# A gated linear unit on one core: the first input tile loaded in one transfer instead of two

## The chip, the cores and the metric

The kernel runs on one core of one Trainium2 chip. The metric is the device time of one execution in microseconds (us). A core has a ScalarE (ACT), a VectorE (DVE), a GpSimd (POOL), a SyncE (SP) and 16 DMA engines that carry data between the chip's memory and the core's on-chip memory. TensorE has no work here.

## The reference

```python
# x: 8192 x 8192, float32
a, b = np.split(x, 2, axis=-1)
return a * (1 / (1 + np.exp(-b)))        # 8192 x 4096, float32
```

So 268.44 MB are read, 134.22 MB are written, and each output element costs one sigmoid and one multiplication.

## The kernel before, in words

The 8192 rows are cut into 32 tiles of 256 rows. In a tile each of the 128 partitions holds two neighbouring rows, so that one partition's share is 64 KB in a row in memory: a tile is 8.39 MB of input and 4.19 MB of output. There are two input buffers (`x_sb0`, `x_sb1`) and two output buffers (`o_sb0`, `o_sb1`); tile i uses buffer i modulo 2 (`SLOTS = 2`).

Three queues set the order of the work, and each is followed strictly in program order, since the helper `place` drops the framework's own dependencies, keeps only the named ones and pins the order:

- **Loads** are issued by SP (`load`, L63). A load of tile i+2 waits for the multiplications of tile i, which had the same input buffer.
- **Sigmoids** run on ACT (L82), in place on the b half of the input buffer.
- **Stores** are issued by ACT too (`store`, L68), in the same queue as the sigmoids. A store waits for the multiplications of its part.

The multiplications (L84) run on VectorE, and for a small share of each tile from tile 2 on, on GpSimd.

`loads`, `works` and `stores` say, tile by tile, into which pieces each step is cut, in eighths of a tile's two rows: (0, 4) is the first row of every partition, (4, 8) the second. A usual tile is loaded and stored whole, and worked in two pieces: 3/16 of the columns of both rows, then the other 13/16. Tile 0 is different: it is loaded in two transfers, one for each row of the pair, worked in four pieces of half a row, and stored in two transfers, one for each row. The last tile is worked in four pieces and stored in three.

`behind[i]` holds stores back in ACT's queue: with 0, the store of the first part stands right behind the sigmoid whose piece completes it; with 1, one further sigmoid is put ahead of that store. Before the change only the last tile has 1.

After the pieces of tile i the load of tile i+2 is issued, then whatever store of tile i is left. For tiles 1 to 31 the first sigmoid also waits until the store of tile i-2 has landed, since it frees the output buffer; the last tile's multiplications wait for that instead, and tile 0 has nothing to wait for but its load.

`_launch_early` moves the first load instruction ahead of the core's opening barrier, so that it is the first thing that SP does; the later loads follow behind the barrier. `_close_on_sync` shortens the closing barrier.

Of the kernel before, what the change touches and what calls it, by code (L numbers as in the profile page):

```python
# [8 lines left out]
def _tiles(ctx, tc, x, out):  # L9
    nc = tc.nc  # L10
    P = nc.NUM_PARTITIONS
    DEP = mybir.DependencyInfo(mybir.DependencyClass.Sync, mybir.DependencyReason.DATA)
    fp32 = mybir.dt.float32
    SIG = mybir.ActivationFunctionType.Sigmoid

    n_rows, n_cols = x.shape
    half = n_cols // 2
    R = 2
    SLOTS = 2
    n_tiles = n_rows // (P * R)  # L20
    x_g = x.rearrange("(g p h r) m -> g h p (r m)", p=P, h=2, r=R)
    out_g = out.rearrange("(g p h r) m -> g h p (r m)", p=P, h=2, r=R)

    pool = ctx.enter_context(tc.tile_pool(name="io", bufs=1))
    xs = [pool.tile([P, R * n_cols], fp32, name=f"x_sb{k}") for k in range(SLOTS)]
    os = [pool.tile([P, R * half], fp32, name=f"o_sb{k}") for k in range(SLOTS)]

    whole = [(0, 8)]
    rows = [(0, 4), (4, 8)]
    cut = half // 16 * 3  # L30
    few_and_most = [(0, 8, 0, cut), (0, 8, cut, half)]
    fourths = [(k, k + 2, k % 4 * half // 4, (k % 4 + 2) * half // 4) for k in range(0, 8, 2)]
    loads = [whole] * n_tiles
    works = [few_and_most] * n_tiles
    stores = [whole] * n_tiles
    behind = [0] * n_tiles
    loads[0] = stores[0] = rows
    works[0] = works[-1] = fourths
    stores[-1] = [(0, 4), (4, 6), (6, 8)]
    behind[-1] = 1  # L40

    def meet(a, b):
        return a[0] < b[1] and b[0] < a[1]

    traced = [[] for _ in range(SLOTS)]
    load_of, mul_of, store_of = {}, {}, {}

    def place(i, ins, *needs):


        kept = {n.ins.name for n in needs}
        for e in traced[i % SLOTS]:
            if e.ins.name not in kept:
                tc.declare_no_dep(ins.ins, e.ins, reason="follows from the waits that are kept")
        traced[i % SLOTS].append(ins)
        tc.keep_in_program_order(ins)
        return ins

    def load(i):
        for lo, hi in loads[i]:  # L60
            c = slice(lo * n_cols // 4, hi * n_cols // 4)
            free = [m for w, m in mul_of.get(i - SLOTS, []) if meet(w, (lo, hi))]
            ins = nc.sync.dma_start(out=xs[i % SLOTS][:, c], in_=x_g[i // 2, i % 2, :, c])  # L63
            load_of.setdefault(i, []).append(((lo, hi), place(i, ins, *free)))

    def store(i, lo, hi):
        c = slice(lo * half // 4, hi * half // 4)
        ins = nc.scalar.dma_start(out=out_g[i // 2, i % 2, :, c], in_=os[i % SLOTS][:, c])  # L68
        done = [m for w, m in mul_of[i] if meet(w, (lo, hi))]
        store_of.setdefault(i, []).append(((lo, hi), place(i, ins, *done)))  # L70

    def work(i, lo, hi, near, far):

        rows = xs[i % SLOTS].rearrange("p (r h m) -> p r h m", r=R, h=2)
        packed = os[i % SLOTS].rearrange("p (r m) -> p r m", r=R)
        r, c = slice(lo // 4, (hi + 3) // 4), slice(near, far)
        b = rows[:, r, 1, c]
        landed = [s for w, s in load_of[i] if meet(w, (lo, hi))]
        gone = [s for w, s in store_of.get(i - SLOTS, []) if meet(w, (lo, hi))]
        by_sigmoid = 0 < i < n_tiles - 1  # L80
        needs = [*landed, *(gone if by_sigmoid else ())]
        sig = place(i, nc.scalar.activation(out=b, in_=b, func=SIG), *needs)  # L82
        engine = nc.gpsimd if far == cut and i > 1 else nc.vector
        mul = engine.tensor_mul(out=packed[:, r, c], in0=rows[:, r, 0, c], in1=b)  # L84
        if by_sigmoid:
            for s in gone:
                tc.add_manual_dep(sig.ins, s.ins.name, DEP, reason="frees the output slot")
        place(i, mul, sig, *(() if by_sigmoid else gone))
        mul_of.setdefault(i, []).append(((lo, hi), mul))

    for i in range(SLOTS):
        load(i)
    for i in range(n_tiles):
        due = list(stores[i])
        for k, piece in enumerate(works[i]):
            work(i, *piece)
            ready = works[i][k - behind[i]][1] if k >= behind[i] else 0
            while len(stores[i]) > 1 and k < len(works[i]) - 1 and due[0][1] <= ready:
                store(i, *due.pop(0))
        if i + SLOTS < n_tiles:  # L100
            load(i + SLOTS)
        for lo, hi in due:
            store(i, lo, hi)
# [71 lines left out]
@with_exitstack  # L175
def kernel(
    ctx: ExitStack,
    tc: tile.TileContext,
    x: bass.AP,
    out: bass.AP,  # L180
):
    nc = tc.nc
    with ExitStack() as pools:
        _tiles(pools, tc, x, out)
    tc.close()
    tc.compile()
    _launch_early(nc)
    _close_on_sync(nc)
# [30 lines left out]
```

## Time and profile before

| | |
|---|---|
| time, median of 3 runs | 932.53 us (932.44 to 932.56) |
| the profiled execution, its own time | 932.5 us |
| its span in the profile | 931.1 us |
| instructions in the span | 325 |
| busy: VectorE, ACT, GpSimd | 25%, 25%, 11% of the span |
| read, written | 268.44 MB, 134.22 MB |
| mean DMA rate over the span | 432 GB/s |

Times in the profile count from the start of the span; the 1.4 us between the span and the execution's time lie outside of what is recorded. A queue is named by its issuer: q1 carries the loads that SP issues, q10 the stores that ACT issues. A DMA's "landing" is the moment at which its completion is seen by whoever waits for it. The profile's packets are the pieces into which a transfer is split for the DMA engines.

### The profile page before, as it was taken

The numbers are of one execution on the slowest core, as the hardware profiler recorded it, in microseconds if no ns is written. First come the engines' busy times: TensorE is split into PE (matmuls) and PEld (weight loads), VectorE is DVE, ScalarE is ACT, GpSimd is POOL, SyncE is SP. The second block draws the span as 40 slices with busy tenths as digits, with TensorE's granted clock in tenths as the row PEclk, the third lists the DMA queues.
The fourth block names the chain that finished last, engine by engine and source line by source line (L and its number), as shares of the span: only waits on it lengthen the run. The fifth ranks groups of instructions, "written<-read, shape, count | busy, mean of one in ns | idle before, by whom it ended". The sixth has DMA issues, their size and how long they took to land.

```text
span 931.1 us, 325 instructions
## 1 busy us (share of the span) xinstructions
DVE 232.5 (25%) x39; ACT 229.8 (25%) x69; POOL 99.9 (11%) x33
## 2 busy tenths in 40 slices
DVE  1133311333113331133320333203332033320233
ACT  2123332033320333203332023320233302333023
POOL 0001111011110111101111011110111101111010
DMA  9999999999999999999999999999999999999998
GB/s 405 450 439 417 428 450 424 455 405 428 450 428 450 407 469 409 428 450 427 452 405 450 428 428 450 424 452 408 428 450 428 450 408 465 411 428 450 427 452 383
DMA packets 9793, 402.67 MB, mean 432 GB/s; under 512 B 1088, under 2 KB 1088, under 8 KB 1088
## 3 DMA queue, kind: packets, MB, share of 16 engines
q1 hardware_dynamic: 4752, 268.44, 66.6%
q10 hardware_dynamic: 5040, 134.22, 33.4%
q14 instruction: 1, 0.01, 0.0%
HBM read 268.44 MB, written 134.22 MB: 432 GB/s over the span
## 4 chain that ended last, share of the span: by engine, by line
DMA 75%; DVE 12%; ACT 12%; issue 0%; ACTq 0%; SPq 0%
DMA out_dram<-o_sb 65%; DVE o_sb L84 12%; ACT x_sb L82 12%; DMA x_sb<-in_x_dram 10%; ACTq L68 0%; SPq L63 0%
## 5 line engine op out<-in xcount | busy, mean ns | idle before, releaser
L84 DVE TENSOR_TENSOR o_sb<-x_sb 128x6656 f32<-128x6656 f32 (+2 forms) x39 | 232.5, 5970 | 690.2 <-ACT x_sb L82 690.2
L82 ACT ACTIVATE x_sb<-x_sb 128x1536 f32<-128x1536 f32 (+1 forms) x68 | 228.5, 3407 | 689.9 <-DMA out_dram<-o_sb 630.0
L84 POOL TENSOR_TENSOR o_sb<-x_sb 128x1536 f32<-128x1536 f32 x29 | 99.7, 3437 | 787.7 <-ACT x_sb L82 787.7
L82 ACT ACT_TABLE_LOAD x1 | 1.3, 1283 | 0.8 <-PEq L203 0.8
L203 POOL MEMSET const-float32-0.0<- 128x1 f32 x1 | 0.1, 98 | 0.2 <-issue 0.2
L203 POOL MEMSET const-bfloat16-1.0<- 128x1 bf16 x1 | 0.1, 101 | 0.0
L203 POOL MEMSET const-uint8-127<- 128x1 uint8 x1 | 0.1, 101 | 0.0
L203 POOL MEMSET const-float32-1.0<- 128x1 f32 x1 | 0.1, 98 | 0.0
## 6 DMA issues: line engine op xcount, KB each, us to landing
out_dram<-o_sb ACTq DMA_DIRECT2D x30, 4096.0 KB, 43.6
x_sb<-in_x_dram SPq DMA_DIRECT2D x2, 4096.0 KB, 16.4
out_dram<-o_sb ACTq DMA_DIRECT2D x3, 2048.0 KB, 28.0
out_dram<-o_sb ACTq DMA_DIRECT2D x2, 1024.0 KB, 8.3
x_sb<-in_x_dram SPq DMA_DIRECT2D x31, 43.5
```

Source lines behind the costliest of these rows:

```text
L82: sig = place(i, nc.scalar.activation(out=b, in_=b, func=SIG), *needs)
L84: mul = engine.tensor_mul(out=packed[:, r, c], in0=rows[:, r, 0, c], in1=b)
L203: nc = _bacc.Bacc("TRN2", target_bir_lowering=False, num_devices=1)
```

## The change

```diff
     stores = [whole] * n_tiles
     behind = [0] * n_tiles
-    loads[0] = stores[0] = rows
+    stores[0] = rows
+    behind[0] = 1
     works[0] = works[-1] = fourths
```

Tile 0 is now loaded whole, in one transfer of 8.39 MB in place of two of 4.19 MB. Its four pieces of work and its two stores stay. With `behind[0] = 1`, the store of its first row stands behind the third sigmoid of tile 0 in ACT's queue, where it stood behind the second. `_launch_early` takes the first load that it finds, which is now the whole tile. Nothing else in the program's order is different: SP has one instruction less, and on ACT the third sigmoid and the first store change places.

## The prediction

> **What bounds the kernel now.** I read the page's DMA rows first, then the timeline of the first 75 us, then the DMA issues one by one with their time to landing, and the end of the trace last.
>
> ```profile
> DMA  9999999999999999999999999999999999999998
> DMA packets 9793, 402.67 MB, mean 432 GB/s; under 512 B 1088, under 2 KB 1088, under 8 KB 1088
> q1 hardware_dynamic: 4752, 268.44, 66.6%
> q10 hardware_dynamic: 5040, 134.22, 33.4%
> ```
>
> The two queues fill 66.6% + 33.4% = 100% of the 16 DMA engines' span. No slice is empty, not even the first or the last. So the bound is the number of bytes, and an edit that keeps the bytes can cost time only if it lets the DMA engines run dry, or changes how long they take for a piece.
>
> The piece: 33 loads made 4752 packets, 144 each. All 68 transfers made 1088 tiny ones, 16 each (completions). So a transfer is 128 data pieces, eight for each DMA engine, one for each partition.
>
> ```profile
> 11.98 3.71 ACT L82 ACTIVATE x_sb<-x_sb 128x2048 f32<-128x2048 f32 x2 [9.91 <-DMA x_sb<-in_x_dram]
> 18.45 0.37 ACTq L68 DMA_DIRECT2D out_dram<-o_sb  x1
> 21.68 3.71 ACT L82 ACTIVATE x_sb<-x_sb 128x2048 f32<-128x2048 f32 x2 [5.99 <-DMA x_sb<-in_x_dram]
> 23.62 4.49 DVE L84 TENSOR_TENSOR o_sb<-x_sb 128x2048 f32<-128x2048 f32 x2 [5.21 <-ACT x_sb L82]
> 28.15 0.36 ACTq L68 DMA_DIRECT2D out_dram<-o_sb  x1
> 46.29 7.12 ACT L82 ACTIVATE x_sb<-x_sb 128x1536 f32<-128x1536 f32 x2 [20.90 <-DMA x_sb<-in_x_dram]
> 60.57 0.36 ACTq L68 DMA_DIRECT2D out_dram<-o_sb  x1
> 70.71 7.12 ACT L82 ACTIVATE x_sb<-x_sb 128x1536 f32<-128x1536 f32 x2 [17.30 <-DMA out_dram<-o_sb]
> ```
>
> Rows 0 and 1 of tile 0 land at 11.98 and 21.68, tile 1 at 46.29; tile 2 starts at 70.71, and what it waits for is a store. The DMA issues at 18.45, 28.15 and 28.15:
>
> ```profile
> out_dram<-o_sb ACTq DMA_DIRECT2D x1, 2048.0 KB, 28.0
> ...
> out_dram<-o_sb ACTq DMA_DIRECT2D x1, 2048.0 KB, 42.5
> x_sb<-in_x_dram SPq DMA_DIRECT2D x1, 42.3
> ```
>
> Store 0a (first row of tile 0) lands at 18.45 + 28.0 = 46.4, just as load 1 does. Store 0b and load 2 land at 28.15 + 42.5 = 70.7 and 70.5. Load and store land in pairs although one is 8.39 MB and the other 2.10: an engine takes one piece from each queue in turn. A pair of these takes 70.5 - 46.3 = 24.2 us (10.49 MB, 433 GB/s), a pair of load and whole store 99.66 - 70.71 = 28.95 us (12.58 MB, 435 GB/s). Hence, over eight pieces, 0.6 us for a 16 KB store piece, 1.2 for 32 KB, 2.42 for a 64 KB load piece. The trace's packet records have 0.611, 1.213 and 2.418. These three durations carry the rest.
>
> In the steady state a tile's sigmoids and products (99.66 to 113.99) take 14.33 us of each 28.95 us, and the DMA has the other buffer's 28.95 us queued meanwhile. That is 14.6 us of cover.
>
> **The change part by part.**
>
> *One load for two.* Per DMA engine, sixteen 32 KB pieces of 1.213 us (19.41) become eight of 64 KB at 2.418 (19.34), with one completion less (0.01): **-0.07 us** of DMA time. The first pieces are slow (1.67 to 2.02 us in the packet records, some 0.6 us of warm-up); the new first piece should pay the same, and I bound the difference by 0.3 us either way, half of it.
>
> *The wait that is added.* No part of tile 0 can start before 21.68 - 0.07 = 21.61. The first sigmoid, first product and store 0a, which had 11.98, 13.92 and 18.45, now queue behind a wait of 9.6 us more. On ACT: sigmoids at 21.61, 23.4 and 25.2, the third done at 27.1. Store 0a waits for product 2, which ended at 23.62 + 4.49 = 28.11 where it followed the same landing: issue at 28.15 - 0.07 = 28.08, **9.6 us later**. Behind it on ACT stands sigmoid 4: 28.08 + 0.37 of issue + 0.04 = 28.5, done 30.4. Product 4 takes 30.4 to 32.7, and load 2 on SP and store 0b on ACT leave at 32.75, **4.6 us later** than 28.15. What hides both delays is load 1, which runs from about 21.2 to beyond 40.
>
> *What is late next.* The question is whether the DMA engines have work at every moment. The ledger, in work per engine: loads 0 and 1 last until 1.0 (first piece) + 0.6 + 2 x 19.34 = 40.3. Load 2 and store 0 (29.0 us) are in the queue by 32.75 and carry it to 69.3. Load 3 and store 1 are issued when tile 1 is done: load 1 lands earlier than 46.29, near 42.8, because it shares with fewer store pieces, and 42.8 + 14.3 = 57.1. They carry it to **98.6**. Then load 4 and store 2 must be there, issued when tile 2 is done, and tile 2 waits for all of store 0. This is the one tight place.
>
> *When store 0 lands.* The load queue is never empty meanwhile, so its 16 pieces alternate with 64 KB ones. Before, its first piece started at 23.6 and tile 2's sigmoid at 70.71, 47.1 us later; that distance stays. So I need only when the first piece of store 0a gets in. It can only do so between load 1's pieces, which begin at about 21.1, 23.5, 25.9, 28.4, 30.8, **33.2, 35.6, 38.0**. Before, it got in 5.1 us after issue, with three load pieces started in between (18.7, 19.9, 21.1 in the packet records). If the delay is a time, or so many bytes already taken in hand, 28.08 + 5.1 gives 33.2. If it is three pieces whatever their size, 35.6. One more piece would be 38.0. I take 33.2, the answer of two of the readings, and keep the others.
>
> From 33.2: tile 2's sigmoid at 80.3 (before: 70.71), load 4 and store 2 issued 14.33 later at 94.65. The first load's piece started 1.0 us after its issue, so they are at the engines by 95.7, 2.9 us before these run dry. **Cost 0.** From 35.6: 82.7, 97.05, 98.05, and with 0.6 us of warm-up 98.65 against 98.6: cost 0 to 0.1, up to 1.3 if a start takes 2.2 us instead of 1.0.
>
> *After that.* Load 3 and store 1 have landed by 98.6, or some pieces later where load 4 mixes in, at worst about 104; 14.3 us on, load 5 and store 3 are issued by 118, and the queue holds until 127.6. From there the old rhythm with its cover. At the end, the last load lands at 911.66 and the first store of tile 31 goes out at 918.13, 6.5 us later; store 30's 9.7 us cover that with 3.2 us to spare. Loads that run a little ahead of stores leave more stores for the end, so this cover grows.
>
> **Sum:** span 931.1 - 0.07 = 931.0; with the 1.4 us outside it, 932.4 against this execution's 932.5. Against the median 932.53: **932.46 us**.
>
> [...]
>
> **The rivals.**
>
> *Slower: the DMA engines run dry at 98.6.* Price: the first piece of store 0a at 38.0 puts tile 2 at 85.1, load 4 and store 2 at 99.45, their first pieces at 100.45; 1.85 us dry and 0.6 of warm-up, 2.5 us: **934.9**. It decides from a first piece later than about 36. For it: the delay was 5.1 us where a bare start took 1.0, so pieces are taken in hand ahead of time, and these are now twice as long. Against: it needs 9.9 us of delay.
>
> *Faster: a transfer has a fixed cost in DMA time.* Row 0 landed at 11.98, row 1 only 9.70 later; if the 2.28 us difference were paid by every transfer in line, one less gives **930.2**. Against: 4.19 MB in 9.70 us are 432 GB/s, the mean of the span, so nothing was paid between the two.
>
> *Slower by the whole delay.* The chain of waits starts with compute on tile 0, and 9.6 us of later start would be **942.1**. It needs DMA engines that idle; the ledger leaves no such place beyond 98.6.
>
> *The change does nothing to the order.* SP's list in the new build has one load of 128x16384 for two of 128x8192, and ACT's three sigmoids ahead of the first store. So it does what it says.
>
> **How the numbers follow.** First piece at 33.2: 0.55, 932.46. At 35.6: 0.29, 932.5 to 933.8. At 38.0: 0.12, 934.9. Whole delay: 0.01. Fixed cost saved: 0.03. Taking 0.2% (1.9 us) as what a measurement of this kernel can tell from no change, the first two are the same: same 0.84, slower 0.13, faster 0.03. The range takes in these two with the warm-up's bound: 932.1 to 934.0; what it leaves out is 0.16.
>
> **What would show it.** Right: one load issue less and 144 packets less on q1 (4608); tile 0's first sigmoid at 21.6, tile 1's near 42.8 (before 46.29), tile 2's near 80.3 or 82.7 (before 70.71), still waiting for a store; no empty DMA slice around 98. Wrong: tile 2 at 85 or later and a gap in DMA there; or a last load that lands with less than 6.5 us of stores behind it, which would open a gap at the end.

## The result, and the profile after

The changed kernel takes **951.73 us** (median of six executions, 950.62 to 960.37), the kernel before 932.58 on the same chip: 19 us slower where no change was forecast, a ratio of 1.0218 over all executions (95% interval 1.0203 to 1.0233; the two medians alone give 1.0205). The profiled execution is the longest of the six (960.37, span 959.0; the other five lie between 950.6 and 952.3), so its profile shows the loss some 9 us larger than usual.

From the page of the changed kernel, the lines that answer to those shown of before:

```profile
DMA  9999999999999999999999999999999999999996
GB/s 435 415 437 408 425 429 424 428 425 422 413 436 428 424 414 427 420 429 415 428 428 416 432 425 406 421 418 435 420 422 428 418 425 426 413 420 426 418 424 294
DMA packets 9649, 402.67 MB, mean 420 GB/s; under 512 B 1072, under 2 KB 1072, under 8 KB 1072
q1 hardware_dynamic: 4608, 268.44, 66.9%
q10 hardware_dynamic: 5040, 134.22, 32.5%
```

The page of before has this for the rate:

```profile
GB/s 405 450 439 417 428 450 424 455 405 428 450 428 450 407 469 409 428 450 427 452 405 450 428 428 450 424 452 408 428 450 428 450 408 465 411 428 450 427 452 383
```

The same bytes, 144 packets less on q1, and DMA engines as busy as before, but at 420 GB/s in place of 432. The loss is spread over the whole span; only the last slice (294) stands out. Two equal stretches from the middle of the kernels, in the table by windows (DVE, ACT and POOL busy, clock, share of the DMA engines, GB/s); first before, then after:

```profile
320.00:900.00 580.00, 141.85 (x20) 142.44 (x40) 68.72 (x20) 1.00 1.00 434
```

```profile
320.00:900.00 580.00, 140.22 (x20) 135.32 (x38) 65.33 (x19) 1.00 1.00 422
```

The share is 1.00 in both: the engines never ran out of work there, so pieces took longer. In the view of the waits this shows as one line that grew by 28.8 us, 1 us for each tile; first before, then after:

```profile
ACT x_sb L82 <- DMA out_dram<-o_sb: 630.0, 29, 22.1
ACT x_sb L83 <- DMA out_dram<-o_sb: 658.8, 29, 29.2
```

The timeline of the start, against the lines that the prediction shows:

```profile
21.98 5.51 ACT L83 ACTIVATE x_sb<-x_sb 128x2048 f32<-128x2048 f32 x3 [19.92 <-DMA x_sb<-in_x_dram]
...
28.45 0.38 ACTq L69 DMA_DIRECT2D out_dram<-o_sb  x1
...
33.13 0.36 ACTq L69 DMA_DIRECT2D out_dram<-o_sb  x1
45.39 7.12 ACT L83 ACTIVATE x_sb<-x_sb 128x1536 f32<-128x1536 f32 x2 [14.61 <-DMA x_sb<-in_x_dram]
...
81.72 7.12 ACT L83 ACTIVATE x_sb<-x_sb 128x1536 f32<-128x1536 f32 x2 [29.21 <-DMA out_dram<-o_sb]
...
96.05 0.36 ACTq L69 DMA_DIRECT2D out_dram<-o_sb  x1
```

Each of these steps came within 2.6 us of the forecast, and nothing ran dry at 98.

**Which pieces took longer.** The trace's packet records give each piece's duration. A load piece that takes longer than 2.418 us is called stretched here. Summed and divided by 16 engines, pieces took 931.4 us before and 953.0 after. 22.0 us of the latter are load pieces beyond their 2.418 us (1.0 before); store pieces are 0.6 us beyond theirs. The stretch begins with load 4 or 5 and is 0.5 to 1.0 us for each tile, mostly in the second and third of a load's eight pieces. The records are followed from the end of one piece to the start of the next, which tells the 16 engines apart. The starts of one load on the engines, 0.3 to 0.6 us apart through all of before, drift from 1.3 us apart (load 4) to 11.6 (load 31). So at the end engines that are ahead have nothing to do while the landing waits for the last one: in the windows table of after,

```profile
925.00:938.00 13.00, 0.00 (x0) 0.00 (x0) 0.00 (x0) 1.00 0.99 429
938.00:946.00 8.00, 4.52 (x3) 5.51 (x3) 0.00 (x0) 1.00 0.41 176
```

Up to 9 us of an engine's time are lost in that gap, 4.9 us in the mean. 21.5 us of longer pieces and 4.9 of gaps make 26.4 of the 27.9 by which the span grew.

**What differs in the queues.** The records of one engine at the border of two tiles (start in us; L and S are load and store pieces, Lm and Sm the 9 ns completion markers, a dash the next tile's):

```
before  240.17 L   242.58 S   243.79 Lm  243.80 Sm  243.80 L'  246.22 S'  247.43 L'
after   126.12 S   127.33 Lm  127.34 S   128.55 L'  130.96 Sm  130.97 L'  133.40 S'  134.60 L' (3.32 us)
```

In these records an engine goes to the other queue after each piece, where that queue has work; what it takes from one queue before it does so is called a turn here. A marker uses up a turn like a piece: at 127.33 the load's marker, at 127.34 the store's next piece. Before, both transfers end in the same pair and the next two begin together. After, the load's marker has used up a turn, the next load is already at its first piece when the store's last has gone, and from there on **loads stand one turn ahead of stores**, on 11 of the 16 engines at load 5. As a number: the last piece of the store ends 1.2 us behind that of the load in before, and 2.4 us behind it in after (median of the engines, each tile from 4 to 30). The other five engines keep the order of before (1.2 us) up to the last tiles, and they are not spared: from load 9 on their load pieces lose 19 to 23 us, those of the eleven 14 to 17. So what slows a piece is not decided by the order of its own engine's two queues alone; the loss is on all 16 engines. The five are also the late ones of the 11.6 us. In the runs rows_behind1 and whole_behind0 below, where all 16 engines stand one turn ahead, load pieces lose 16.8 and 17.3 us and the gap at the end is 1.2 and 0.8.

### The profile page after: what moved, and what is told of

It is laid out like the page before. It is cut to its first block, busy times and chain, and to the rows that moved or that the text cites. A ratio compares the mean times of both kernels' runs of the same rounds, so it can differ in the third digit from the quotient of the medians.

```text
span 959.0 us, 324 instructions
## 1 busy us (share of the span) xinstructions
DVE 232.5 (24%) x39; ACT 229.8 (24%) x69; POOL 99.9 (10%) x33
## 2 busy tenths in 40 slices
DMA packets 9649, 402.67 MB, mean 420 GB/s; under 512 B 1072, under 2 KB 1072, under 8 KB 1072
## 4 chain that ended last, share of the span: by engine, by line
DMA 75%; DVE 12%; ACT 12%; issue 0%; ACTq 0%; SPq 0%
DMA out_dram<-o_sb 66%; DVE o_sb L85 12%; ACT x_sb L83 12%; DMA x_sb<-in_x_dram 9%; ACTq L69 0%; SPq L64 0%
```

## The experiments

Theory at first: load 4 reached the engines just as store 1 ended (99.4 us), and this meeting set the engines on two different orders. Rivals: the large first transfer sets them apart; or loads ahead of stores are enough. In the diffs `...` leaves out what is unchanged.

**Half of the change, and three ways around the meeting.** rows_behind1 has only the second half:

```diff
     loads[0] = stores[0] = rows
+    behind[0] = 1
```

> The kernel before with only the second half of the change: tile 0 is still loaded in two rows, and its first store stands behind the third sigmoid. Store 0a leaves some 5 us later than before (near 23.6), so stores run about three pieces behind loads, alike on all engines; load 4 leaves near 90 and the load queue is never empty. Theory (after the change the load queue ran empty while store 1 still ran, load 4 reached the engines just as store 1 ended at 99.4, and the engines went on in two different orders): no such meeting here, 932.5 us, pieces not stretched. Rival 'the large first transfer sets the engines apart from the start': also 932.5. Rival 'loads that run ahead of stores by a fixed number of pieces are enough': stretched pieces, 945 to 955.

951.64 us (ratio 1.0205, 1.019 to 1.022). The first store left at 21.82 and got in at 26.2 instead of 23.6: one load piece later. Loads stand one turn ahead (2.4 us) from tile 3 on; 16.8 us of stretched pieces. In load 4, whose first pieces still start within 0.3 us of each other, the stretch has begun (0.4 us), so the drift of the engines follows it and doesn't cause it. No large first load, no meeting, the same loss: the theory of the meeting and the rival of the first load fall.

whole_whole stores tile 0 whole too:

```diff
-    stores[0] = rows
-    behind[0] = 1
```

> The changed kernel, but tile 0 is also stored whole (and behind[0] is 0 again): store 0 leaves near 33 in pieces of 32 KB, gets in with about one piece of load 1 to go, and lands near 66. Tile 2 then waits for its load, not for store 0, near 71, load 4 leaves near 86 and the load queue is never empty. Theory (the meeting of load 4 with the end of store 1 divides the engines): no meeting, 932.5. Rival 'the large first transfer sets the engines apart': as the changed kernel, 950 to 952. Rival 'a fixed lead of loads over stores is enough': here stores lead by about a piece, so it expects 932.5 unless a lead of either kind counts.

934.62 us (1.002, 1.0011 to 1.0029). Loads come out three turns behind stores (store's end 8.5 us before the load's), and the waits say the same: all 32 are for loads.

```profile
ACT x_sb L81 <- DMA x_sb<-in_x_dram: 692.8, 32, 22.1
```

1.8 us of stretched pieces, nearly all at the start. The 2 us that it is slower are a gap of its own: the last load lands late (its sigmoid starts at 915.81, before at 911.66), store 30 is gone at 921 on most engines, and the first store of tile 31 leaves at 922.28.

tile2_short works tile 2 in fourths (`works[2] = fourths`), tile2_long puts one more instruction on ACT in tile 2:

```diff
+        extra = []
+        if i == 2 and far == half:
+            a = rows[:, r, 0, c]
+            extra = [place(i, nc.scalar.activation(out=a, in_=a, func=mybir.ActivationFunctionType.Copy), *needs)]
         sig = place(i, nc.scalar.activation(out=b, in_=b, func=SIG), *needs)
...
-        place(i, mul, sig, *(() if by_sigmoid else gone))
+        place(i, mul, sig, *extra, *(() if by_sigmoid else gone))
```

> The changed kernel with tile 2 worked in fourths on VectorE alone, as tile 0 is: load 4 and store 2 leave some 3 us earlier after tile 2's first sigmoid (near 92.7 instead of 96.05) and reach the engines near 96, while store 1 still has some three pieces to go. Theory (it is the coincidence of load 4's arrival with store 1's end that divides the engines): all engines take the same order, 932.5 to 933.5. Rival 'the large first transfer': 950 to 952. Rival 'a fixed lead of loads is enough': loads still lead by a piece, 945 to 955.

> The changed kernel with one more ACT instruction in tile 2, a copy in place of the a half (5.73 us, as the sigmoid of that shape): load 4 and store 2 leave near 101.8 and reach the engines near 105, when they have been dry since 99.5, so all restart together. Theory: 5.5 us dry and 0.6 of warm-up, no stretched pieces afterwards, 938 to 939, so more work makes the kernel faster than the changed one. Rival 'the large first transfer': the loss stays and the delay comes on top, 951 to 957. Rival 'a fixed lead of loads is enough': the restart takes the lead away, 938 to 939 too.

tile2_short: 951.73 us, loads one turn ahead, 16.1 us stretched: a second miss for the meeting. tile2_long: 937.04 us (1.0048). The engines ran dry at 99.2 for 2 to 3 us (5.5 were expected), restarted together with load and store in the same pair (1.2 us), and no later tile is stretched. **More work on ACT made the changed kernel 15 us faster.** What is left of the three is the order of the two queues.

whole_behind0 has the other half of the change alone (tile 0 loaded whole, `behind[0]` stays 0).

> The first half of the change alone: tile 0 is loaded whole and behind[0] stays 0. Store 0a still waits for product 2 and leaves near 28.3, load 2 and store 0b near 35. Theory (it is the late first store, by whatever edit, that puts loads a turn ahead of stores): loads end one turn ahead, as with both halves, 948 to 955. Rival 'the third sigmoid ahead of the first store is what does it': 932.5 to 934.

952.63 us, one turn ahead, 17.3 us stretched. Either half alone costs what both cost.

**Shifting the queues by one marker.** In the middle of a kernel one transfer is split in two across the partitions, which keeps bytes and pieces and adds a marker to its queue. Of before_cut_store8 (before_cut_load10, after_cut_load6 and after_cut_store6 differ in the tile and in which of the two queues):

```diff
+    load_cut, store_cut = None, 8
+    def cuts_of(i, tile):
+        return [slice(0, 112), slice(112, P)] if i == tile else [slice(0, P)]
...
-        ins = nc.scalar.dma_start(out=out_g[i // 2, i % 2, :, c], in_=os[i % SLOTS][:, c])
+        for p in cuts_of(i, store_cut):
+            ins = nc.scalar.dma_start(out=out_g[i // 2, i % 2, p, c], in_=os[i % SLOTS][p, c])
```

> The kernel before, with one edit in its middle: the store of tile 8 goes out as two transfers, of partitions 0 to 111 and 112 to 127, the same bytes and still eight data pieces for each engine, but one more completion marker (9 ns) in the store queue. If markers take turns as pieces do, stores fall one turn behind loads from there on, as after the change. Theory 'loads one turn ahead of stores': from about tile 10 on load pieces are stretched by 0.5 to 0.8 us a tile and the engines drift apart, 943 to 951. Rival 'the way in which tile 0 starts': no effect, 932.5 to 932.9. Rival 'a split transfer is itself slow': one tile's worth, under 2 us.

949.2 us (1.0175, 1.0159 to 1.019). The kernel before, with its two row loads, becomes nearly as slow as the changed one by one more marker of 9 ns on each engine and a split store whose own pieces lose 2.3 us. Store ends follow load ends by 2.4 us from tile 11 on. From then on load pieces are stretched (12.7 us in all), and the rate falls at the split, in the middle of the trace (the table by windows):

```profile
100.00:280.00 180.00, 42.56 (x6) 48.71 (x14) 24.07 (x7) 1.00 1.00 432
280.00:320.00 40.00, 12.05 (x2) 7.92 (x3) 3.44 (x1) 1.00 1.00 409
320.00:910.00 590.00, 137.81 (x21) 142.45 (x40) 68.74 (x20) 1.00 1.00 426
```

> The kernel before, with the load of tile 10 (which leaves together with the store of tile 8) split in the same manner: one more marker in the load queue, so stores get one turn ahead. Theory 'loads one turn ahead': stores ahead do no harm (as where tile 0 was stored whole), 932.5 to 934. Rival 'any shift of one turn between the queues does it': 943 to 951. Rival 'the way in which tile 0 starts': 932.5 to 932.9.

949.46 us, a miss, and not for the reason of the rival: 14.3 us are lost in the split load itself, and the tiles after it, with loads one turn behind (-2.4 us), have 0.5 us of stretch in all.

> The changed kernel, with the load of tile 6 split in the same manner: one more marker in the load queue takes away the one turn that loads are ahead. Theory 'loads one turn ahead': stretched pieces up to about tile 6 only, 1 us of them at the start and 0.5 to 0.9 for each of two or three tiles, 934 to 937. Rival 'the first load, or the meeting near 99 us, has set the engines apart for good': 950 to 952.

975.85 us, a clear miss. The split load cost 12.2 us. The lead was gone as meant (1.2 us), but the stretch went on, at 0.7 to 1.4 us a tile and at two places in each. Here the engines are 3.3 us and more apart from each other, about one turn of each queue (2.42 + 1.21). Such a distance alone does no harm: after its split before_cut_load10 has 3.3 to 3.7 us of it and 0.5 us of stretch in all. So what counts is neither the order within an engine alone nor the distance alone.

> The changed kernel, with the store of tile 6 split in the same manner: one marker more in the store queue, so loads get two turns ahead instead of one. Theory 'loads ahead of stores': the loss stays, 948 to 956. Should only a lead of exactly one turn do harm: 934 to 938. Rival 'a split transfer mends it by whatever disturbance it makes': 934 to 937, as with the split load.

938.16 us (937.1 to 950.8). Loads came two turns ahead (6.0 us), and the stretch, 0.4 to 0.7 us up to tile 8, fell to 0.02 from tile 10 on. Two of the 16 engines got only to one turn ahead; from load 9 on they lost 5.5 and 3.9 us, each of the others at most 1.2. That fits the other theory of this expectation (the time is 0.2 us above its range): here **exactly one turn** does harm, two do not.

> The kernel before, with the store of tile 8 in three transfers (partitions 0 to 95, 96 to 111, 112 to 127): two more markers in the store queue, so loads get two turns ahead instead of one. With one marker it took 949.2. Theory 'any lead of loads over stores': 945 to 952. Theory 'a lead of one turn only' (in the run with one marker more in the changed kernel the stretching ended at a lead of two turns): a few us for the split itself and no stretched pieces after it, 933 to 938.

Three transfers (partitions 0 to 95, 96 to 111, 112 to 127), two markers more: 936.72 us (1.0043), two turns ahead (6.0 us) from tile 11 to 30, 1.4 us of stretch in all. With one marker 949.2, with two 936.7, though the split disturbs more: one turn it is. Most of the 4 us that are left lie at the split store, whose pieces lose 3.2.

**Where the stretching comes from.** after_tiles_in_a_row lays tiles out one after another, after_same_input reads the first tiles' rows again and again:

```diff
-    x_g = x.rearrange("(g p h r) m -> g h p (r m)", p=P, h=2, r=R)
+    x_g = x.rearrange("(g h p r) m -> g h p (r m)", p=P, h=2, r=R)     # out_g likewise
```
```diff
-... in_=x_g[i // 2, i % 2, :, c])
+... in_=x_g[0, i % 2, :, c])
```

> The changed kernel with another layout of the tiles over the rows: tile i takes 256 rows in a row, so neighbouring partitions are 64 KB apart in x instead of 128, and 32 KB apart in the output instead of 64. Queues, pieces and their order are the same. Theory 'the stretching comes from where in memory the pieces lie that are read and written at the same time': it changes much, 932.5 to 940 or above 960. Theory 'it comes from the order of the queues alone': the same stretching, 948 to 955.

> The changed kernel, but every tile loads the input rows of tile 0 or 1 (by its parity), so only tiles 0 and 1 of the output hold what the reference has. The order of the queues is the same. Theory 'each tile pays for reaching rows that were not read before': no stretching after the first tiles, 932.5 to 936. Theory 'order of the queues': 948 to 955. Theory 'it depends on how far apart in memory reads and writes lie': now a different distance for each tile, so the stretching varies from tile to tile.

952.12 and 952.59 us, one turn ahead, 17.8 and 18.4 us stretched: neither half the distance between rows nor reading the same rows again makes a difference.

Between seven and nine tenths of the stretch lie in pieces beside ACT's sigmoids at the start of a tile, so the compute engines were the next suspects. after_no_gpsimd has `engine = nc.vector` for all products; after_little_sigmoid also works on 64 columns of a piece only:

```diff
-        sig = place(i, nc.scalar.activation(out=b, in_=b, func=SIG), *needs)
+        few = rows[:, r, 1, slice(near, near + 64)]
+        sig = place(i, nc.scalar.activation(out=few, in_=few, func=SIG), *needs)
```

> The changed kernel without GpSimd: VectorE multiplies all pieces. Loads should again get one turn ahead. Theory 'the stretching comes from the DMA queues alone': 948 to 955 as before. Theory 'from GpSimd's access to the on-chip memory at the start of a tile': no stretched pieces, 932.5 to 936.

952.02 us, 16.5 us stretched: not GpSimd.

> The changed kernel without GpSimd, and with each sigmoid on the first 64 columns of its piece only, so most of the output is a product with no sigmoid in it; ACT's 7.1 us at the start of a tile become some 0.5 us, VectorE's products stay. Loads and stores of a tile leave some 5 us sooner after its landing, in the same order. Theory 'the DMA queues alone': loads one turn ahead and 945 to 955. Theory 'ACT's access to the on-chip memory beside the load pieces': no or much weaker stretching, 932.5 to 938.

933.57 us (1.001) and 1.7 us stretched, but the run tells nothing of ACT: with the shorter work loads came to stand three turns ahead (9.7 us). It is one more case of a lead other than one that does no harm. To hold the lead at one, the last two runs have the split store of before_cut_store8, no GpSimd, and little work: cut_little_sigmoid as above, cut_little_work also for the products:

```diff
-        r, c = slice(lo // 4, (hi + 3) // 4), slice(near, far)
+        r, c = slice(lo // 4, (hi + 3) // 4), slice(near, near + 64 if i > 1 else far)
```

> The kernel before with the store of tile 8 in two transfers (949.2 us by itself), without GpSimd, and with each sigmoid on the first 64 columns of its piece only, so most of the output has no sigmoid in it. The marker puts loads one turn ahead whatever the compute takes. Theory 'the DMA queues alone': stretched load pieces from tile 12 on as in that run, 943 to 951. Theory 'ACT's work beside the load pieces': none, 933 to 938.

937.17 us, inconclusive: loads were two turns behind before the split and one behind after it; 2.2 us stretched.

> The same, and from tile 2 on sigmoids and products both work on 64 columns of a piece only, so most of the output of these tiles is what the buffer held from tiles 0 and 1; after tile 1 the engines are all but idle and loads and stores leave some 1 to 2 us after a tile's landing. Theory 'the DMA queues alone': the stretching stays, 943 to 951. Theory 'compute engines' work beside the load pieces', ACT's or VectorE's: none, 933 to 938.

949.78 us (1.0184, 1.0169 to 1.0199): one turn ahead from tile 11 on, 13.2 us stretched, as with all the work, although ACT and VectorE did 10 us each in 590 (the table by windows):

```profile
100.00:280.00 180.00, 3.45 (x14) 3.35 (x14) 0.00 (x0) 1.00 1.00 431
...
320.00:910.00 590.00, 9.87 (x40) 10.17 (x40) 0.00 (x0) 1.00 1.00 425
```

So the stretch doesn't need the compute engines' work.

**A way out for the whole first load.** after_rows_tile2 loads tile 2 in rows, so its queue takes nine turns more:

```diff
-    stores[0] = rows
+    stores[0] = loads[2] = rows
```

> The changed kernel with the load of tile 2 in two rows: sixteen pieces and two markers for each engine in place of eight and one, so the load queue uses nine more turns and stores come out some four turns ahead. Theory 'only loads exactly one turn ahead do harm': 932.5 to 934.5, the whole loss gone. Rival 'the late first store sets the engines apart for good': 948 to 955.

935.58 us (1.0031, 1.0019 to 1.0043), 1 us over the expectation: loads three turns behind (-8.5 us), no stretch after the start, and 2.7 us of gap at the end, as in whole_whole. The loss of the change is gone by an edit that leaves its first load as it is. No version came below the kernel before.

All runs by how far loads stand ahead of stores in the steady state:

| turns ahead | runs (median us) | stretched load pieces, us per engine |
|---|---|---|
| 3 | after_little_sigmoid 933.6 | 1.7 |
| 2 | before_cut_store8_thrice 936.7; after_cut_store6 938.2 (14 of 16 engines) | 1.4; 5.2 |
| **1** | changed kernel 951.7 (11 of 16 engines); rows_behind1 951.6; whole_behind0 952.6; tile2_short 951.7; after_tiles_in_a_row 952.1; after_same_input 952.6; after_no_gpsimd 952.0 | 22.0; 16.8; 17.3; 16.1; 17.8; 18.4; 16.5 |
| **1** from tile 11 | before_cut_store8 949.2; cut_little_work 949.8 | 12.7; 13.2 |
| 0 | before 932.6; tile2_long 937.0 | 1.0; 2.9 |
| 0, engines a turn apart | after_cut_load6 975.9 | 41.7, of it 12.2 in the split load |
| -1 | before_cut_load10 949.5; cut_little_sigmoid 937.2 | 15.8, of it 14.3 in the split load; 2.2 |
| -3 | whole_whole 934.6; after_rows_tile2 935.6 | 1.8; 1.7 |

Stretch is that of the profiled execution. **What stays open** is what in the DMA engines or in memory makes a load piece take up to 3.8 us in place of 2.4 when loads stand one turn ahead. The compute work is not needed for it (13.2 us of stretch with 10 us of work on ACT and VectorE each), and neither the second layout of the tiles nor reading the same rows changed it (17.8 and 18.4 us). That the order on an engine alone does not set the time of its pieces is shown by the five engines of the changed kernel that keep the old order and are slowed most (19 to 23 us); what the 16 engines have in common there, and why a lead of one turn does it (16.1 to 22.0 us) and one of two does not (1.4), no run shows.

## Why the prediction was wrong, point by point

- **The bound** (bytes through the DMA engines): right. DMA share stays 1.00 and 402.67 MB are moved; what changed is the time of a piece, which the prediction named as the second way to lose time and then did not price: a term put at nothing without a reason.
- **One load for two, -0.07 us:** too small to be seen here.
- **The wait that is added:** right. 9.6 us later for store 0a was forecast; it left at 28.45, 10.0 later. Load 2 and store 0b: 4.6 forecast, 33.13 against 28.15 is 5.0.
- **When store 0 lands:** right. The first piece got in at 33.4 (33.2 taken); tile 2 began at 81.72 (80.3), load 4 left at 96.05 (94.65). Tile 1 began at 45.39, not 42.8; load 1's pieces were stretched by 1.0 us.
- **The tight place at 98.6:** the sum held, no engine stood still. The first piece of load 4 came at 99.4, 3.3 us after issue and not 1.0, nor the 2.2 of its dearer case, so the 2.9 us to spare were used up. The ledger adds up both queues, and so it couldn't show that the load queue alone was empty from 94.6 to 99.4, while stores went on to 100.6. (Its own terms, 69.3 + 29.0, make 98.3 and not 98.6; nothing hangs on the 0.3.)
- **"After that. [...] From there the old rhythm with its cover": this is the step that failed.** The cover was there, the rhythm was not. The ledger counted pieces and took 0.611, 1.213 and 2.418 us for constants, because before has no other values after its start. But before shows only one order of the queues, load and store in the same pair. The change put loads one turn ahead, and in the runs with that order from the first tiles on load pieces are stretched by 16 to 22 us, where before has 1.0. The prediction had even said that loads would run ahead, and took that for an advantage.
- **The end** ("this cover grows"): wrong. With the engines 11.6 us apart a load lands when the slowest is done, and the others stood idle, in the profiled execution 4.9 us in the mean of the 16 (rows_behind1 1.2, whole_behind0 0.8).
- **The rivals:** the slower one had the right sign, at the wrong place: it priced a dry spell at 98.6, not a lasting change of the rate, and the highest price of any rival was 942.1. A dry spell (tile2_long, 937.0) would have been the better outcome.
- **"An engine takes one piece from each queue in turn":** right, the records shown above have it so, and this was the part that mattered. The prediction counted a completion as time alone (0.01 us). In the records a completion marker takes 9 ns and a turn; one marker more, with its split store, cost 16.6 us (before_cut_store8).

## What to carry to other kernels

Where a kernel is bound by transfers, as this one is, don't stop at a ledger of bytes: write down, from the packet records, in which order the queues take turns, and ask what the edit does to that order for the rest of the run. Here a small edit at the start (19 us slower), or one completion more in one queue (16.6), shifted two streams against each other, and the lead that the first tiles set stayed, on nearly every engine, to the last ones. Where the engines are fully busy and the rate is lower, as here (share 1.00, 422 GB/s in place of 434), look for pieces that take longer before looking for gaps. In this kernel a shift to two or more turns (before_cut_store8_thrice, 936.7 where one turn took 949.2) or a short dry spell (tile2_long, 937.0 where the changed kernel took 951.7) took most of the loss away.

## What the runs showed of the hardware that was not expected

- Away from starts and split transfers, load pieces of 64 KB take 2.418 us with loads and stores in the same pair, with loads two or three turns ahead, or one to three behind (but see after_cut_load6). With most engines' loads one turn ahead, one or two of a load's eight pieces are clearly stretched, in the changed kernel's profile to 2.9 us in the median (of the 654 over 2.5 from load 4 on) and to 3.8 at most, and the five engines in the old order are slowed with the rest (19 to 23 us from load 9 on).
- Two transfers that joined busy engines got in later: 5.1 us from issue to the first piece for store 0a of before (three load pieces began meanwhile), 3.3 at load 4 of after, against 1.0 where the engines were idle (the first load, and load 4 of tile2_long).
- A load of 8.39 MB split over 112 and 16 partitions cost 12.2 and 14.3 us by itself, a store split in this way far less (before_cut_store8_thrice, 4 us in all).
